# Output projection of ten token tiles in pairs by Strassen's scheme: seven block products for eight, block sums on GpSimd and VectorE

## The chip, the cores and the metric

The kernel runs on one core of a Trainium2 chip. A core has a matrix engine (TensorE, PE in the profile, with its weight loads listed apart as PEld), a vector engine (VectorE, DVE), an activation engine (ScalarE, ACT), GpSimd (POOL) and SyncE (SP), which here only issues transfers. SBUF is the on-chip memory of 128 partitions; PSUM is where TensorE writes, in eight banks that each hold 128x512 numbers in float32. The metric is the time of one execution on the device in microseconds, as the median of several runs.

## The reference

One decoder layer on 2048 tokens of width 1024. The input is normalised, projected once, and goes through two kinds of attention with eight heads each (a causal one with a forget gate, a sliding-window one). Each branch is multiplied by a SiLU gate path; the two halves of 512 columns are joined, sent through one output projection, normalised, and added to the input through a gate:

```
proj = h @ w_in[l]
qa, ka, va, fa, za, qb, kb, vb, zb = jnp.split(proj, split_points, axis=-1)
oa = forgetting_attention(qa, ka, va, fa + b_fgate[l])
oa = oa * jax.nn.silu(za)
...
ob = ob * jax.nn.silu(zb)
y = jnp.concatenate([oa, ob], axis=-1) @ w_out[l]
x = x + gate[:, None, :] * rms_norm(y, g_post[l])
```

All inputs and the output are float32.

## The kernel before

**Number format.** TensorE multiplies float16. Each float32 operand is scaled and split into a high and a low float16 limb, and a product is three matmuls: high by high, high by low, low by high. All of them add into one PSUM bank.

**Stages.** First the input is normalised and transposed, and the projections for the window attention run, with that attention beside them. Then comes the sweep of the forgetting attention: eight heads of 20 steps, 160 in all, each with scores (L1294 to L1297), an exponential (L1301), its split in limbs (L1305, L1308) and the product with the values (L1318 to L1321). Between the steps, in the same loop, the remaining projections are put in as filler. The gate projections za (for the forgetting attention) and zb (for the window attention) are evacuated by `evac_z` (L352): a Tanh on ACT, a multiply on DVE, and a transfer to `z_d` in DRAM from POOL's queue. `w_done` (L277) computes for each of the eight blocks of 128 columns the factor `fac8` by which its z is off. The attention results go to `o_d` in DRAM.

**Output projection.** It is done for 16 token tiles of 128 rows by the class `Out`. `load` brings o and z of a tile, `turn` (L1406) transposes o by eight PE transposes, multiplies it with z from the banks (`gate`, L1419), takes the sum of squares (L1423) and from it a scale (`root_scale`, L118, a power-of-two-like estimate of an inverse root with an exponent offset 15), and makes the high limb on ACT (L1437) and the low limb on DVE (L1438). `product(n, k)` (L1476) does one of eight k blocks of one half n of 512 output columns: three matmuls at L1489. After the eighth, `evac` multiplies the bank by the inverse scale and the gate row `gacc` on DVE (L1498) and sums its squares on ACT (L1499); after both halves, `root` and `store` (L1507 to L1519) finish the norm, add x and store the tile. The last half of the last tile is done in two pieces (`last`, L1440).

The weights `w_out` are loaded in 16 pieces during the sweep and split into limbs in `wohl` (`w_out_load`, `w_out_split`, L1387 and L1388), each row block scaled by `wsc`, which holds its `fac8` times a common factor. The right half's float32 pieces stay in `hT[3]`.

**Order.** The order within each engine is written out by hand. `ounits` is the list of units of the output projection, a unit being one `product` (three matmuls) or one `turn`; `ofill` runs them in turn. `after(n, f)` puts f off by n ticks, and outside the sweep a tick comes every second unit (`tick2`). 33 units (`N_IN`: both halves of tiles 0 and 1, and the turn of tile 2) are filler in the last head of the sweep; the rest follow the sweep at L1645. A tile's load is started two tiles ahead.

**Buffers.** Five PSUM banks `bk` take turns (`bank`, `release`); the sweep holds the other three. `Ts[0]` holds o and z of two tiles each in the tail, `Ts[1]` the limbs of the last head's q and k; `hT[2]` holds x and y of two tiles. The area for the descriptors of POOL's transfers has its default size.

Of the kernel before, what the change touches and what calls it, by code (L numbers as in the profile page):

```python
# [18 lines left out]
P = 128  # L19
# [22 lines left out]
def hybrid_layer(  # L42
# [75 lines left out]
    def root_scale(dst, ss):  # L118

        h = small.tile([P, 1], I32, tag="rs_h", name="sc_h")  # L120
        V.tensor_scalar(h[:], ss.bitcast(I32), 1, None, op0=ALU.logical_shift_right)
        V.tensor_scalar(dst.bitcast(I32), h[:], -1, 0x5F3759DF + (15 << 23), op0=ALU.mult, op1=ALU.add)
# [42 lines left out]
    fac8 = const.tile([P, KT], F32, name="fac8")  # L165
    wrt = const.tile([P, 1], F32, name="wrt")
# [986 lines left out]
    ps_st = fox_pool("ps_st", 1, space=PSUM)  # L1153
    ps_po = fox_pool("ps_po", 1, space=PSUM)
    ps_bx = fox_pool("ps_bx", 1, space=PSUM)
    bk += [ps_bx.tile([P, CH], F32, name=f"bk{n}") for n in (3, 4)]
# [198 lines left out]
    def open_out():  # L1355
# [7 lines left out]

        fm = sm(1, "w_p2")
        V.tensor_reduce(fm[:], fac8[:], axis=AX.X, op=ALU.max)
# [24 lines left out]
    oio = {}  # L1390

    class Out:
# [47 lines left out]
        def last(self, k):  # L1440
# [3 lines left out]
            if k == 0:  # L1444
                self.x = xy(self.t % 2)
# [30 lines left out]
        def product(self, n, k):  # L1476
# [3 lines left out]
            if k == 0:  # L1480
# [3 lines left out]
                else:  # L1484
                    self.x = xy(self.t % 2)
# [8 lines left out]
            def evac():  # L1494
                if n == 0:
                    self.y = xy(2 + self.t % 2)
# [23 lines left out]

    outs = [Out(t) for t in range(NB)]

    ounits, oloads = [], {}
    for t, n in [(0, 0), (1, 0), (0, 1), (1, 1)] + [(t, n) for t in range(2, NB) for n in range(2)]:
        if n == 0 and t + 2 < NB:
            oloads[len(ounits)] = t + 2
        for q in range(KT):
            ounits.append(lambda t=t, n=n, q=q: outs[t].product(n, q))
            nxt = 2 if (t, n) == (0, 1) else t + 1 if n == 0 and 2 <= t < NB - 1 else None
            if q == 2 and nxt:  # L1530
                ounits.append(lambda nxt=nxt: outs[nxt].turn(4))
    opos = [0]
    N_IN = 4 * KT + 1

    def ofill(n, each=None):
        for _ in range(n):
            if opos[0] in oloads:
                outs[oloads[opos[0]]].load()
# [5 lines left out]
    with tc.manual_schedule():  # L1544
# [30 lines left out]
        for s, stp_ in enumerate(steps):  # L1575
# [43 lines left out]
            if not opened and pos[0] >= N_OPEN and (r >= 14 or not late):  # L1619
# [8 lines left out]
                w_out_load(0)  # L1628
            if hd == 7 and r in (4, 6):
# [14 lines left out]
        fxs.close()  # L1644
        ofill(len(ounits) - opos[0], tick2)  # L1645
        for _ in range(4):
            tick()

    foxo.close()
# [32 lines left out]
```

## Time and profile before

| | |
|---|---|
| runs, us | 1195.15, 1192.07, 1190.61 |
| median of the runs, us | 1192.07 |
| span of the profiled execution, us | 1188.7 |
| PE busy in it, us (share) | 1147.3 (97%) |
| DVE busy, us (share) | 914.1 (77%) |
| ACT busy, us (share) | 665.9 (56%) |
| POOL busy, us (share) | 115.2 (10%) |

The profile is of one execution, whose span is 3.4 us under the median of the runs. A group of instructions is shown as line, engine, operation, output<-input, shapes and count, then the busy time in us and the mean duration of one in ns, then the idle time of the engine in front of them and what ended it. Matmuls are pipelined: one of 512 columns lasts some 380 ns from its start to its end, and the next starts before it is done, so the chain of waits, which follows the end of each, gives the time per matmul. "L1489" is a line of the kernel.

### The profile page before, as it was taken

To read this page: it belongs to the slowest core of one execution; us is meant where nothing else is said; L and a number is where in the kernel's file an instruction comes from. 1 tells how busy PE (TensorE), PEld (TensorE's weight loads), DVE (VectorE), ACT (ScalarE), POOL (GpSimd) and SP (SyncE) were. 2 spreads that over 40 slices of the span, in tenths; PEclk is the share of its full clock that TensorE was granted. 3 is DMA by queue.
4 is the path that set the end of the run, shared out by engine and by line. 5 is a ranking of instruction groups with operands and counts; after the bars stand their busy time and mean duration, and the time that the engine had idled before them with its cause. 6 is when DMAs were issued, how large, how long until landed. Compare 5 with 4: busy or idle time off the path is not lost.

```text
span 1188.7 us, 27244 instructions
## 1 busy us (share of the span) xinstructions
PE 1147.3 (97%) x10853; PEld 693.6 (58%) x10853; DVE 914.1 (77%) x2263; ACT 665.9 (56%) x1102; POOL 115.2 (10%) x231
## 2 busy tenths in 40 slices
PE   5899999999999998999999999999999999999997
PEld 2475556765558976555555555555555555555554
DVE  7876678687776748688888889887888887766665
ACT  2784345464655521476766667666666778433332
POOL 2000112212121211001000101001000000000000
PEclk9899999999999999999999999999999999999999
DMA  9745433314223322413325322212311345455642
GB/s 333 277 121 87 84 89 99 61 59 109 83 70 88 58 63 63 65 50 95 68 70 72 102 63 60 50 48 71 48 42 39 92 127 176 147 171 184 198 167 96
DMA packets 87579, 120.22 MB, mean 101 GB/s; under 512 B 27508, under 2 KB 63388, under 8 KB 87452
## 3 DMA queue, kind: packets, MB, share of 16 engines
q1 hardware_dynamic: 76184, 85.69, 24.4%
q0 software_dynamic: 10832, 32.50, 13.2%
q8 instruction: 85, 1.39, 0.6%
q14 instruction: 42, 0.34, 0.1%
q10 hardware_dynamic: 436, 0.28, 0.1%
HBM read 71.04 MB, written 25.18 MB: 81 GB/s over the span
## 4 chain that ended last, share of the span: by engine, by line
PE 79%; DVE 10%; DMA 6%; issue 2%; ACT 2%; SPq 1%; DVEq 0%; ACTq 0%
PE bk L317 29%; PE bk L1489 13%; PE bk L335 7%; PE sta L1295 4%; PE sta L1294 4%; PE bk L1245 4%; PE poa L1320 2%; PE poa L1321 2%; PE poa L1318 2%; DMA wa<-in_w_ada_dram 2%; PE pxb L888 2%; PE pss L855 2%; PE pob L907 2%; DVE a_m L1248 1%; PE bk L1410 1%
## 5 line engine op out<-in xcount | busy, mean ns | idle before, releaser
L1301 ACT ACTIVATE p<-sta,lift,scl_qk 128x1024 f32<-128x1024 f32 (+2 forms) x160 | 172.0, 1075 | 143.7 <-PE sta L1295 88.2
L317 PE MATMUL bk<-hT,wh_qk 128*128 128x512 f16 x768 | 195.3, 380 | 0.0
L1248 DVE TENSOR_REDUCE a_m<-bk 128x1 f32<-128x512 f32 x192 | 130.5, 686 | 55.2 <-PE bk L1245 54.0
L1308 DVE TENSOR_TENSOR pha<-p,pha 128x1024 f16<-128x1024 f32 (+2 forms) x160 | 169.1, 1057 | 0.2 <-ACT pha L1305 0.2
L1489 PE MATMUL bk<-wohl,oz 128*128 128x512 f16 x744 | 167.0, 379 | 0.7 <-DVE oz L1438 0.7
L1305 ACT ACTIVATE pha<-p 128x1024 f16<-128x1024 f32 (+2 forms) x160 | 148.1, 926 | 5.4 <-PE poa L1321 0.7
L1489 PEld LDWEIGHTS <-oz 128*128 128x128 f16 x744 | 71.9, 99 | 79.4 <-DVE oz L1438 2.8
L317 PEld LDWEIGHTS <-wh_qk 128*128 128x128 f16 x768 | 72.5, 98 | 78.2 <-issue 6.6
L1321 PE MATMUL poa<-vt,pha 128*128 128x65 f16 x1088 | 116.1, 192 | 1.4 <-DVE pha L1308 1.2
L1318 PE MATMUL poa<-vt,pha 128*128 128x65 f16 x1088 | 116.5, 193 | 0.5 <-DVE ona L1327 0.4
L1320 PE MATMUL poa<-vt,pha 128*128 128x64 f16 x1088 | 116.5, 194 | 0.0
L1245 PE MATMUL bk<-T 66*128 66x512 f16 (+2 forms) x320 | 110.2, 350 | 3.1 <-DVE a_m L1248 3.0
L1294 PE MATMUL sta<-T 128*128 128x512 f16 (+1 forms) x320 | 110.9, 346 | 2.5 <-ACT p L1301 2.4
L1318 PEld LDWEIGHTS <-pha 128*128 128x128 f16 x1088 | 101.5, 96 | 15.1 <-DVE ona L1327 1.5
L1295 PE MATMUL sta<-T 69*128 69x512 f16 (+1 forms) x320 | 109.8, 348 | 0.0
L1320 PEld LDWEIGHTS <-pha 128*128 128x128 f16 x1088 | 100.9, 97 | 11.4
L1321 PEld LDWEIGHTS <-pha 128*128 128x128 f16 x1088 | 100.8, 99 | 1.8 <-DVE pha L1308 1.7
L317 PE MATMUL bk<-hT,wh_za 128*128 128x512 f16 x384 | 99.7, 378 | 0.0
L335 PE MATMUL bk<-wh_va,hT 128*128 128x128 f16 x1536 | 90.7, 219 | 0.0
L335 PEld LDWEIGHTS <-hT 128*128 128x128 f16 x1536 | 87.5, 98 | 4.7 <-issue 2.1
L317 PE MATMUL bk<-hT,wh_zb 128*128 128x512 f16 x384 | 88.9, 379 | 0.0
L317 PE MATMUL bk<-hT,wh_qb 128*128 128x512 f16 x384 | 87.4, 379 | 0.0
(498 smaller groups left out, 1860.4 us busy)
## 6 DMA issues: line engine op xcount, KB each, us to landing
hT<-in_x_dram SPq DMA_DIRECT2D x20, 512.0 KB
wa<-in_w_ada_dram SPq DMA_DIRECT2D x16, 512.0 KB
z_d<-tz POOLq DMA_DIRECT2D x32, 256.0 KB, 2.9
T<-stq SPq DMA_DIRECT2D x64, 128.0 KB
T<-o_d SPq DMA_DIRECT2D x16, 512.0 KB
T<-z_d SPq DMA_DIRECT2D x16, 512.0 KB
out_dram<-hT SPq DMA_DIRECT2D x15, 512.0 KB
xt<-in_x_dram SPq DMA_DIRECT2D x12, 512.0 KB
```

The source lines that it names most:

```text
L317: PE.matmul(ps, whl[:, a, k, :], hT[ci][:, b, k, :], start=(k == 0 and n == 0), stop=(k == KT - 1 and n == 2))
L335: PE.matmul(ps[:, u * P:(u + 1) * P], hT[ci][:, a, k, u * P:(u + 1) * P], whl[:, b, k, :], start=(k == 0 and n == 0), stop=(k == KT - 1 an ...
L1245: PE.matmul(mx[:, :w], T[0:XM, 0, i * P:(i + 1) * P], T[0:XM, 2, pc * CH:pc * CH + w], start=True, stop=True)
L1294: PE.matmul(self.st[:, o:o + w], T[:, 3, kb_], T[:, 1, qc], start=True, stop=False)
L1295: PE.matmul(self.st[:, o:o + w], T[0:XR, 2, kb_], T[0:XR, 0, qc], start=False, stop=not diag)
L1301: A.activation(self.p32[:, :self.w], self.st[:, :self.w], AF.Exp, scale=scl[f"qk{self.hd}"][:], bias=lift[:])
L1305: A.activation(self.ph[:, 0, :self.w], self.p32[:, :self.w], AF.Copy)
L1308: V.tensor_tensor(self.ph[:, 1, :self.w], self.p32[:, :self.w], self.ph[:, 0, :self.w], op=ALU.subtract)
L1318: PE.matmul(po[:, u, :], ph[:, 0, pq], vt[:, b, hd, 0:65], start=(self.first and n == 0 and u == 0), stop=False)
L1320: PE.matmul(po[:, u, 0:64], ph[:, 0, pq], vt[:, b, hd, 65:VW], start=False, stop=False)
L1321: PE.matmul(po[:, u, :], ph[:, 1, pq], vt[:, b, hd, 0:65], start=False, stop=(self.last and n == len(self.blocks) - 1))
L1489: PE.matmul(py, self.hl[:, i, k, :], w_slot(8 * j + k)[:, cc], start=(k == 0 and m_ == 0), stop=(k == KT - 1 and m_ == 2))
```

## The change

Token tiles 4 to 13 are taken in five pairs. A pair is a 256 x 1024 matrix of gated attention results, cut into 2 x 2 blocks (tile 2p or 2p+1; first or second 512 of the inner columns), and `w_out` is cut into 2 x 2 blocks of 512 x 512. The eight block products become seven, in the form with seven sums after them:

- sums of the weights, once: T1 = B12 - B11, T3 = B22 - B12, T2 = B22 - T1, and T4 (with its sign turned), on POOL, 128x1024 at a time (`t_add`). For them the left half of `w_out` is loaded again into `Ts[1]` once the last scores are done (`t_load`), and the limbs of the four results are made by ACT and DVE (`t_high`, `t_low`) and kept where the values of the attention were.
- sums of the left side, per pair: four of 128x512 on POOL (`sums`).
- products 1, 2, 6, 7, 5, 3, 4 of four k blocks each, three matmuls per k block (`product` of the class `Two`).
- sums of the results: product 1 and 5 are copied from their banks by ACT; the others are added to a float32 row block by DVE; two sums that need only copies are made by POOL (`fives`). The gate row is multiplied in by POOL (`gated`) after the squares.

The sums over rows of z need both halves of the inner columns to have one scale per row of `w_out` blocks; so each za block is multiplied by the ratio `rat` of its factor to that of the matching zb block, by POOL, before it goes to `z_d`. Offsets 15 become 14 in `root_scale` since sums are larger. The tail gets the three banks that the sweep held. The descriptor area of POOL's transfers is set to 8192 bytes, which makes room for the new buffers. The units and what goes between them are listed at fixed unit numbers (`oat`).

```diff
-    def root_scale(dst, ss):
+    def root_scale(dst, ss, e=14):
...
-        V.tensor_scalar(dst.bitcast(I32), h[:], -1, 0x5F3759DF + (15 << 23), op0=ALU.mult, op1=ALU.add)
+        V.tensor_scalar(dst.bitcast(I32), h[:], -1, 0x5F3759DF + (e << 23), op0=ALU.mult, op1=ALU.add)
...
+            if kind == "za":
+                t = sm(1, "w_p2")
+                V.reciprocal(t[:], fac8[:, n + 4:n + 5])
+                V.tensor_tensor(rat[:, n:n + 1], fac8[:, n:n + 1], t[:], op=ALU.mult)
...
                 V.scalar_tensor_tensor(t[:], t[:], 1.0, ps, op0=ALU.add, op1=ALU.mult)
                 free()
+                if kt < 4:
+                    G.tensor_scalar(t[:], t[:], rat[:, kt:kt + 1], None, op0=ALU.mult)
                 G.dma_start(z_d[kt, :, ci * CH:(ci + 1) * CH], t[:])
...
-        V.tensor_scalar(wsc[:], fac8[:], ysc[:], None, op0=ALU.mult)
+        for n in range(2):
+            V.tensor_scalar(wsc[:, 4 * n:4 * n + 4], fac8[:, 4:8], ysc[:], None, op0=ALU.mult)
...
+    def t_add(n, h):
+
+        a = slice(h * 2 * CH, (h + 1) * 2 * CH)
+        b = slice((h + 2) * 2 * CH, (h + 3) * 2 * CH)
+        dst, x0, x1 = {1: (Ts1f[:, a], hT3f[:, a], Ts1f[:, a]), 3: (hT3f[:, a], hT3f[:, b], hT3f[:, a]),
+                       2: (hT3f[:, b], hT3f[:, b], Ts1f[:, a]), 4: (Ts1f[:, b], Ts1f[:, b], hT3f[:, b])}[n]
+        G.tensor_tensor(dst, x0, x1, op=ALU.subtract)
...
+        def sums(self):
...
+            G.tensor_tensor(c[:, 0:4], z1[:, 0:4], z1[:, 4:8], op=ALU.add)
+            G.tensor_tensor(f[:, 0:4], c[:, 0:4], z0[:, 0:4], op=ALU.subtract)
+            G.tensor_tensor(f[:, 4:8], z0[:, 0:4], z1[:, 0:4], op=ALU.subtract)
+            G.tensor_tensor(c[:, 4:8], z0[:, 4:8], f[:, 0:4], op=ALU.subtract)
...
+        def product(self, m, k):
+            n, half = {1: (0, 0), 2: (0, 1), 6: (1, 0), 7: (1, 1), 5: (2, 0), 3: (2, 1), 4: (3, 1)}[m]
...
+                PE.matmul(py, self.h[n][:, i, 4 * half + k, :], w,
+                          start=(k == 0 and m_ == 0), stop=(k == 3 and m_ == 2))
...
+        def add(self, dst, m, other):
+            V.tensor_tensor(dst, bk[self.bank[m]][:], self.u[other], op=ALU.add)
+            release(self.bank[m])
...
+        def fives(self):
+            G.tensor_tensor(self.u[2], self.u[15], self.u[2], op=ALU.add)
+            G.tensor_tensor(self.y(1, 1), self.u[15], self.u[3], op=ALU.add)
...
+        def gated(self, e, h):
+            G.tensor_tensor(self.y(e, h), self.y(e, h), gacc[:, h * CH:(h + 1) * CH], op=ALU.mult)
...
+    def prep(w):
+        i = len(ounits)
+        oat(i - 28, w.load)
+        for e in range(2):
+            oat(i - 18 + 2 * e, w.turn, e)
+            oat(i - 16 + 2 * e, w.gate, e)
+            oat(i - 14 + 2 * e, w.squares, e)
+        oat(i - 12, w.sums)
+        oat(i - 9, w.scale_)
+        for n, (a, b) in enumerate(((-7, -5), (0, 3), (6, 9), (12, 14))):
+            oat(i + a, w.high, n)
+            oat(i + b, w.low, n)
...
+    for n, h, at in ((1, 0, 6), (1, 1, 6), (3, 0, 8), (3, 1, 8), (2, 0, 22), (2, 1, 22), (4, 0, 26), (4, 1, 26)):
+        oat(N_IN + at, t_add, n, h)
+    for m, n in enumerate((1, 3, 2, 4)):
+        for k in range(4):
+            at = N_IN + (12, 20, 30, 38)[m] + 2 * k
+            oat(at, t_high, n, k)
+            oat(at + 1, t_low, n, k)
+    std(2, 0, 3)
...
+    for p in range(2, 7):
+        prep(twos[p])
+        for m in (1, 2, 6, 7, 5, 3, 4):
+            strassen(twos[p], m)
...
+            if s == len(steps) - 2:
+                t_load()
...
+        ps_tl = fox.enter_context(tc.tile_pool(name="ps_tl", bufs=1, space=PSUM))
+        bk += [ps_tl.tile([P, CH], F32, name=f"bk{n}") for n in (5, 6, 7)]
+        order_[:0] = [5, 6, 7]
...
-    nc = _bacc.Bacc("TRN2", target_bir_lowering=False, num_devices=1)
+    nc = _bacc.Bacc("TRN2", target_bir_lowering=False, num_devices=1, dynamic_dma_scratch_size=8192)
```

`std(t, n)` lists the eight units of one half of a tile as before. In `strassen(w, m)` the four units of product m are followed, one unit later, by its copy or sum, the square at three and the gate row at four; `root` comes six units after the last product, the two stores eight and ten after it.

More of the change, by code (lines that the diff above doesn't have):

```diff
@@ L165, in hybrid_layer @@
     fac8 = const.tile([P, KT], F32, name="fac8")
+    rat = const.tile([P, 4], F32, name="rat")
     wrt = const.tile([P, 1], F32, name="wrt")
@@ L1527, in hybrid_layer, with oat, std @@
+    outs = [Out(t) for t in range(NB)]
+    twos = {p: Two(p) for p in range(2, 7)}
+    ounits, oev = [], {}
+    def oat(n, f, *a):
+        oev.setdefault(n, []).append(lambda: f(*a))
+    def std(t, n, nxt=None):
         for q in range(KT):
[L1528 to L1529 removed]
+            ounits.append(lambda q=q: outs[t].product(n, q))
             if q == 2 and nxt:
[L1531 removed]
+                ounits.append(lambda: outs[nxt].turn(4))
@@ new lines, in prep, with strassen, end @@
+    def prep(w):
+        i = len(ounits)
+        oat(i - 28, w.load)
+        for e in range(2):
+            oat(i - 18 + 2 * e, w.turn, e)
[6 more added lines that the diff above has]
+            oat(i + b, w.low, n)
+    def strassen(w, m):
+        for k in range(4):
+            ounits.append(lambda k=k: w.product(m, k))
+        e = len(ounits)
+        def end(e_, h_):
+            oat(e + 3, w.square, e_, h_)
+            oat(e + 4, w.gated, e_, h_)
+        if m == 1:
+            oat(e + 1, w.copy, 1)
+        elif m == 2:
+            oat(e + 1, lambda: w.add(w.y(0, 0), 2, 11))
+            end(0, 0)
+        elif m == 6:
+            oat(e + 1, lambda: w.add(w.u[2], 6, 11))
+        elif m == 7:
+            oat(e + 1, lambda: w.add(w.u[3], 7, 2))
+        elif m == 5:
+            oat(e + 1, w.copy, 5)
+            oat(e + 1, w.load_x)
+            oat(e + 2, w.fives)
+            oat(e + 5, w.square, 1, 1)
+            oat(e + 6, w.gated, 1, 1)
+        elif m == 3:
+            oat(e + 1, lambda: w.add(w.y(0, 1), 3, 2))
+            end(0, 1)
+        else:
+            oat(e + 1, lambda: w.add(w.y(1, 0), 4, 3))
+            end(1, 0)
+            oat(e + 6, w.root)
+            oat(e + 8, w.store, 0)
+            oat(e + 10, w.store, 1)
```

156 lines of the change are left out of this document (143 added, 13 removed).

## The prediction

> **What bounds the kernel now.** I read the head of the page first, then the chain of waits, then the busy time of the engines in three stretches after the attention sweep.
>
> ```profile
> span 1188.7 us, 27244 instructions
> ...
> PE 1147.3 (97%) x10853; PEld 693.6 (58%) x10853; DVE 914.1 (77%) x2263; ACT 665.9 (56%) x1102; POOL 115.2 (10%) x231
> ```
> ```profile
> 600.00:700.00 100.00, 98.67 (x1022) 56.97 (x1018) 87.17 (x184) 65.36 (x75) 9.39 (x14) 1.00 0.36 73
> ...
> 1022.90:1047.60 24.70, 24.70 (x128) 12.63 (x126) 16.79 (x45) 7.60 (x14) 0.00 (x0) 1.00 0.66 216
> 1047.60:1161.30 113.70, 113.70 (x582) 58.28 (x581) 74.88 (x210) 37.99 (x70) 0.00 (x0) 1.00 0.56 186
> ```
>
> The columns are the stretch, its length, then the busy time of PE, PEld, DVE, ACT and POOL, the granted clock, the DMA share and GB/s. From 1022.9 us on only the output projection is left, and PE is busy all the time at the full clock. DVE works 66% of it, ACT a third, POOL not at all. So in this stage a matmul taken away is time taken away, as long as what replaces it stays under PE. The chain of waits, in order of time, gives the price of one tile:
>
> ```profile
> 1022.91 1.94 PE bk L1489 x9
> 1024.85 0.87 PE bk L1410 x8
> 1025.73 3.88 PE bk L1489 x18
> ...
> 1029.72 6.50 PE bk L1489 x30
> 1036.22 0.87 PE bk L1410 x8
> 1037.10 4.53 PE bk L1489 x21
> 1041.63 0.12 PE bk L1427 x2
> 1041.74 5.85 PE bk L1489 x27
> 1047.59 0.87 PE bk L1410 x8
> ...
> 1058.96 0.87 PE bk L1410 x8
> ```
>
> A matmul of 128x512 takes 6.50/30 = 0.2167 us of PE, the eight transposes of a tile 0.87 us, and two tiles 1058.96 - 1036.22 = 22.74 us, without a gap between the pieces.
>
> **What is removed.** A pair of tiles has 2 x 2 x 8 x 3 = 96 matmuls now. By the scheme it has seven products of four k blocks with three limb products each, 84. Five pairs save 60 matmuls of the same shape, 60 x 0.2167 = 13.0 us, and the count at L1489 and its successor together goes from 744 to 684. Transposes and the sum over partitions for the scale keep their number. A pair then needs 22.74 - 12 x 0.2167 = 20.1 us of PE. Tiles 0 to 3, 14 and 15 and the last 27 us of the kernel stay as they are.
>
> **What is added to DVE and ACT per pair.** The groups of the stretch from 1030 us to the end give the durations:
>
> ```profile
> L1498 DVE SCALAR_TENSOR_TENSOR hT<-bk,w_sw,gacc 128x512 f32<-128x512 f32 x27 | 20.1, 746 | 8.2 <-PE bk L1489 8.2
> L1499 ACT ACTIVATE yj<-bk,w_sw 128x512 bf16<-128x512 f32 x27 | 18.6, 687 | 72.8 <-DVE hT L1498 72.8
> L1438 DVE SCALAR_TENSOR_TENSOR oz<-T,w_pw,oz 128x1024 f16<-128x1024 f32 x13 | 16.7, 1282 | 6.5 <-ACT oz L1437 6.5
> L1518 DVE SCALAR_TENSOR_TENSOR hT<-hT,y_rs 128x1024 f32<-128x1024 f32 x13 | 16.5, 1272 | 0.0
> L1419 DVE TENSOR_TENSOR T<-bk,T 128x512 f32<-128x512 f32 x24 | 15.5, 686 | 19.5 <-PE bk L1410 19.5
> L1437 ACT ACTIVATE oz<-T,w_pw 128x1024 f16<-128x1024 f32 x13 | 14.9, 1142 | 1.0 <-DVE w_pw L122 1.0
> L1423 ACT ACTIVATE zj<-T 128x1024 bf16<-128x1024 f32 x12 | 12.7, 1056 | 25.6 <-issue 25.6
> ```
>
> and DVE's timeline (start, duration) shows the root of one tile, 1037.90 to 1040.03, and the four small instructions of the scale, 1041.78 to 1042.44:
>
> ```profile
> 1037.90 0.15 DVE L1509 TENSOR_TENSOR y_ss<-y_ss 128x1 f32<-128x1 f32 x1
> ...
> 1039.87 0.16 DVE L115 SCALAR_TENSOR_TENSOR y_rs<-rs_t,rs_y 128x1 f32<-128x1 f32 x1
> ...
> 1041.78 0.16 DVE L121 TENSOR_SCALAR sc_h<-bk 128x1 int32<-128x1 int32 x1 [0.66 <-PE bk L1427]
> ...
> 1042.44 1.27 DVE L1518 SCALAR_TENSOR_TENSOR hT<-hT,y_rs 128x1024 f32<-128x1024 f32 x1
> 1043.62 1.28 DVE L1438 SCALAR_TENSOR_TENSOR oz<-T,w_pw,oz 128x1024 f16<-128x1024 f32 x1
> ```
>
> DVE: four gates as L1419, 4 x 0.69 = 2.7; low limbs of three and a half tiles as L1438, 3.5 x 1.28 = 4.5; five sums of a bank with a row block, taken as L1419, 5 x 0.69 = 3.4 (the four evacuations of L1498, 3.0, go); two final instructions as L1518, 2.5; the scale 0.66; the root 2.1 now, with some four more small instructions at about 0.19, 2.9. Sum 16.7 us in 20.1. Starts at 1042.44 and 1043.62 lie 1.18 apart where one lasts 1.27, so back to back it is about a tenth of a microsecond less for each of these. ACT: two squares of L1423, 3.5 high limbs of L1437, two copies and four squares as L1499: 2.1 + 4.0 + 1.4 + 2.7 = 10.2 us, about half of the time. Both lie beside PE; DVE's cover is only 3.4 us a pair. DMA moves the same 4 MB per pair (two tiles of o, z, x and out) in 20.1 instead of 22.74 us, 186 x 22.74/20.1 = 210 GB/s, less than the 216 GB/s of the first stretch above.
>
> **What is added to POOL.** Ten two-input instructions of 128x512 a pair, eight of 128x1024 once (the T sums), and a scale of 128x512 for each of 16 z blocks during the sweep. The page of before shows no such instruction on POOL; the nearest rows among its groups are
>
> ```profile
> L508 POOL TENSOR_SCALAR_AFFINE_SELECT bmask<-bm 128x256 f32<-128x256 f32 x1 | 0.4, 401 | 0.1
> ...
> L511 POOL TENSOR_SCALAR_AFFINE_SELECT dm<-zero 128x128 f32<-128x128 f32 x1 | 0.3, 300 | 0.0
> ```
>
> That is 0.79 ns an element over 0.2 us. One input at 512 would be 0.6 us and at 1024 1.0 us, the lower end. I take twice the slope for two inputs, 1.0 and 1.8 us, because the second input must be read too; four times, 1.8 and 3.4 us, is my upper end. A pair then costs POOL 10 us, between 6 and 18, under 20.1 at every end. [...]
>
> What no row shows is how POOL and DVE get along when both read SBUF. If only DVE instructions with two SBUF inputs must take turns with POOL (low limbs 4.5 and finals 2.5, 7.0 us a pair), turns and all come to 10 + 7.0 = 17.0 us, still under PE; if every DVE instruction must, 16.7 + 10 = 26.7, over it. Both ends are kept; I take the first, with 0.4 us of PE stall a pair for a DVE that is late now and then, 2 us in all. [...]
>
> In the sweep DVE is busy 87% (row above) and 16 POOL scales of 0.6 us are spread over some 500 us. Wholly exposed they would be 16 x 0.6 = 10 us; DVE's idle 13% and the two tz buffers cover them, and I take 0.3 us. If the cover were gone, the next Tanh on ACT would wait for its tz. The smaller descriptor area for POOL's DMAs costs nothing unless they are held back; a weight load, by the DMA issues (count, KB, us to landing), lands in
>
> ```profile
> wr_qk<-in_w_in_dram POOLq DMA_DIRECT2D x16, 256.0 KB, 5.4
> ```
>
> and is issued 42 units (of three long matmuls, 0.65 us) ahead, so one or two in flight at a time is enough. The eight reciprocals and products for rat, and two small wsc instructions, go under DVE's idle time.
>
> **The first pair: the T sums.** The extra load of w_out (2 MB) waits for the last scores, and SP then has nothing queued in front; the timelines of PE and SP show the last scores and SP's next transfer:
>
> ```profile
> 1016.94 0.22 PE L1297 MATMUL sta<-dmaskT,identb 128*128 128x128 bf16 x1
> ```
> ```profile
> 1023.62 0.38 SPq L1328 DMA_DIRECT2D o_d<-ona  x1
> ```
>
> So it starts near 1017.2, and at 216 GB/s its first half is in SBUF about 5 us later, before POOL needs it near 1027. T1 and T3 are then done in 4 x 1.8 = 7 us, before ACT and DVE split them. What is tight is DVE. Per T block the splits cost what those of w_out cost:
>
> ```profile
> L1388 DVE SCALAR_TENSOR_TENSOR wohl<-hT,wsc,wohl 128x512 f16<-128x512 f32 x8 | 6.0, 748 | 4.7 <-ACT wohl L1387 4.7
> ```
> ```profile
> 1031.86 1.14 ACT L1437 ACTIVATE oz<-T,w_pw 128x1024 f16<-128x1024 f32 x1
> ```
>
> The first T high limb comes behind this ACT instruction (ends 1033.0) and its low limb on DVE near 1033.7. Up to the low limb that the first pair starts with stand eight T low limbs 6.0, tile 3's low limb 1.28, four gates 2.7, two evacuations 1.5, a root 2.1, a scale 0.66, and that limb itself 1.28: 15.5 us, so 1049.2, or about 1048 with the overlap of starts. PE gets there at 1022.91 + 96 x 0.2167 + 3 x 0.87 + 0.24 = 1046.6, and needs that limb in its third matmul, 1047.0. PE waits 1 to 2 us. Behind it on POOL the pair's sums stand ahead of T2 and T4; at 1.8 and 3.4 us an instruction T2 would come some 3 us late for the third product, at 1.0 and 1.8 in time. I take 2 us for this stage, between 0 and 6.
>
> **Sum.** 1188.7 - 13.0 + 2 + 2 + 0.3 = 1180.0 us of span. The median of the runs is 1192.07, 3.4 over the span, so 1183.4, rounded to 1183.5.
>
> **Rivals.** (1) *All hidden:* PE stays without gaps, as it is now through all 113.70 us, and nothing of the 4.3 us is paid: 1192.1 - 13.0 = 1179.1. For it speaks DVE's 3.4 us of air a pair; against it the 15.5 us queue before the first pair. Chance 0.20. (2) *The forecast,* 1180.5 to 1187: 0.45. (3) *DVE becomes the bound of the pairs:* POOL takes from it 3.4 us a pair and up to 3 more, so a pair lasts 20.1 to 23 us; with 4 us at the T sums 1183 to 1198, centre 1191. For it speaks that DVE would go from 66% to 83% with waits on POOL inside its queue (sums of the next pair stand on POOL ahead of the two fives, for which DVE's sum of the third product waits). Chance 0.18. (4) *DVE and POOL take turns in everything,* the other side: 26.7 us a pair against 22.74, 5 x 4.0 = 20 us, and at the T sums POOL's 8 x 1.8 = 14 us fall on DVE's queue, which is late already, some 10 of them on PE: 1192 + 30 = 1222, or 1200 if half of it is exposed. It decides from 6.0 us a pair (22.74 - 16.7), that is 0.6 us lost per POOL instruction. For it speaks only that no row excludes it. Chance 0.15. (5) *The change doesn't take matmuls away* (a count that stays at 744): 1192; the code leaves little room, 0.02.
>
> **How the numbers follow.** A measurement of this kernel tells about 0.5%, 6 us, from no change: faster is under 1186.1, slower over 1198. Faster: 0.20, nearly all of (2), 0.42, and 0.02 of (3), 0.64. Same: 0.03 of (2), 0.14 of (3), 0.02 of (5), 0.19. Slower: 0.15 of (4) and 0.02 of (3), 0.17. The range, 1177.5 to 1196, holds (1), (2) and most of (3); the forecast's own range is 1180.5 to 1187.
>
> **What would show it.** 684 matmuls of 512 columns at 0.217 us; a pair of 20.1 to 21 us from transposes to transposes; POOL instructions of 128x512 near 1.0 us; PE idle near 1047 released by DVE's low limb, 1 to 3 us; the sweep ending within 1 us of 1022.9. DVE rows as L1438 well over 1.3 us, or PE idle in every pair behind DVE, speak for (3); the same on L1419's kind, with a bank as input, for (4).

## The result and the profile after

Four runs of the changed kernel took 1226.43 to 1231.70 us, median 1228.88; four of the kernel before beside them 1190.61 to 1196.04, median 1193.61. The ratio is 1.0295 (95% interval 1.027 to 1.032): slower by 3%, where 1183.5 us had been forecast and 1177.5 to 1196 was the range. The head of the page of the profiled execution:

```profile
span 1226.0 us, 27290 instructions
## 1 busy us (share of the span) xinstructions
PE 1146.4 (94%) x10793; PEld 688.9 (56%) x10793; DVE 957.3 (78%) x2248; ACT 688.4 (56%) x1138; POOL 239.0 (19%) x305
```

Sixty matmuls are gone (10853 to 10793), 13 us at full clock, yet PE's busy time is less than 1 us under that of before, and the span is 37.3 us longer. In places the granted clock has fallen, to 0.87 in the first of the stretches below, so the same matmuls keep PE busy for longer. The busy times by stretch (columns as in the prediction; the first stretch is from the first matmul behind the sweep to the first product of the first pair, the others lie between the transposes of one pair and those of the next):

```profile
1027.30:1070.30 43.00, 26.10 (x127) 13.09 (x128) 34.68 (x51) 12.71 (x23) 21.59 (x11) 0.87 0.32 101
1079.90:1104.20 24.30, 20.88 (x105) 10.28 (x104) 18.02 (x31) 11.04 (x20) 14.40 (x10) 1.00 0.57 180
1104.20:1130.60 26.40, 22.35 (x105) 10.83 (x104) 19.68 (x43) 10.21 (x18) 14.67 (x11) 0.94 0.48 160
1130.60:1155.40 24.80, 22.26 (x106) 11.02 (x105) 17.34 (x34) 10.14 (x18) 14.47 (x10) 0.93 0.51 170
```

PE, busy without a break before, now stands still for 2 to 4 us in every pair, and no other engine is full: DVE has 17 to 20 us of work in 24 to 26, POOL 14.5, ACT 10 to 11. Where PE waits, its timeline says (three rows from the first stretch and just before it, with the idle time in front and its releaser):

```profile
1026.13 0.20 PE L1329 MATMUL poa<-vt,pha 128*128 128x65 f16 x1 [2.18 <-DVE pha L1316]
...
1037.43 0.38 PE L1440 MATMUL bk<-w_mx,ones 128*128 128x1 f32 x2 [3.30 <-ACT zj L1436]
...
1070.28 1.03 PE L1652 MATMUL bk<-wohl,oh 128*128 128x512 f16 x2 [12.44 <-ACT oh L1631]
```

and its groups behind the sweep show the place in the pairs, the sum over partitions for the scale (L1612):

```profile
L1612 PE MATMUL bk<-wst,ones 128*128 128x1 f32 x20 | 3.9, 263 | 13.7 <-ACT zj L1598 13.7
```

**The 12.44 us.** DVE's timeline in front of it is the root of a single tile, instructions of one number a partition:

```profile
1055.61 0.14 DVE L105 TENSOR_SCALAR rs_v<-rs_v 128x1 f32<-128x1 f32 x1
...
1056.39 2.27 DVE L115 SCALAR_TENSOR_TENSOR rs_y<-rs_t,rs_y 128x1 f32<-128x1 f32 x1
1058.70 2.26 DVE L110 SCALAR_TENSOR_TENSOR rs_t<-rs_y,rs_v 128x1 f32<-128x1 f32 x1
1060.99 2.26 DVE L115 SCALAR_TENSOR_TENSOR rs_y<-rs_t,rs_y 128x1 f32<-128x1 f32 x1
1063.29 2.26 DVE L110 SCALAR_TENSOR_TENSOR rs_t<-rs_y,rs_v 128x1 f32<-128x1 f32 x1
1065.58 0.16 DVE L115 SCALAR_TENSOR_TENSOR y_rs<-rs_t,rs_y 128x1 f32<-128x1 f32 x1
```
```profile
1056.30 4.64 POOL L1552 TENSOR_TENSOR hT<-hT,T 128x1024 f32<-128x1024 f32 x2
1060.90 4.63 POOL L1552 TENSOR_TENSOR T<-T,hT 128x1024 f32<-128x1024 f32 x2
```

An instruction of 0.16 us lasts 2.26. The starts are 2.3 us apart, the length of one of the four T sums that POOL runs at that time: one of DVE's, one of POOL's, in turn. Away from the sums the same lines last 0.16 to 0.22. The instruction at L105 reads one tensor, those that wait read two. Behind this root in DVE's queue stand the scale, a T low limb and an evacuation (L1513). For that evacuation ACT has stood still, and the first pair's high limb, for which PE waits, is behind it on ACT:

```profile
1067.80 0.69 ACT L1514 ACTIVATE yj<-bk,w_sw 128x512 bf16<-128x512 f32 x1 [15.02 <-DVE hT L1513]
...
1069.09 1.14 ACT L1631 ACTIVATE oh<-zx,w_pw 128x1024 f16<-128x1024 f32 x1
```

The other two waits in the list above are of the same kind. The last `pha` of the sweep (L1316, two inputs, 0.55 us as a rule) takes 2.12 while POOL is in the first T sum (2.18 us at 1026.13). Then a final instruction (L1533), a sum of squares (L1524) and one of the root (L110) last 2.25, 2.30 and 1.64 us in place of 1.28, 0.15 and 0.22, and the gate whose squares PE waits for stands behind them (3.30 us at 1037.43).

**The 13.7 us.** DVE and POOL in the fourth pair:

```profile
1151.18 1.88 DVE L1635 SCALAR_TENSOR_TENSOR oz<-sf,w_pw,oz 128x1024 f16<-128x1024 f32 x1 [1.37 <-ACT oz L1631]
1152.99 1.22 DVE L1686 TENSOR_TENSOR a_cv<-a_mr 128x2 f32<-128x2 f32 x1
...
1156.94 1.29 DVE L1693 SCALAR_TENSOR_TENSOR hT<-hT,a_m 128x1024 f32<-128x1024 f32 x1
1158.14 1.28 DVE L1635 SCALAR_TENSOR_TENSOR oz<-sf,w_pw,oz 128x1024 f16<-128x1024 f32 x1
...
1159.94 1.28 DVE L1693 SCALAR_TENSOR_TENSOR hT<-hT,a_m 128x1024 f32<-128x1024 f32 x1
...
1163.59 1.27 DVE L1594 TENSOR_TENSOR zx<-bk,zx 128x512 f32<-128x512 f32 x2
```
```profile
1163.70 0.38 PE L1612 MATMUL bk<-wst,ones 128*128 128x1 f32 x2 [0.57 <-ACT zj L1598]
1166.15 0.38 PE L1612 MATMUL bk<-wst,ones 128*128 128x1 f32 x2 [2.07 <-ACT zj L1598]
```

A low limb and the sum for the root wait for POOL (1.88 and 1.22 us), then come the root, two finals, limbs, and only then the gate of the pair's second tile. The squares follow it, and PE stands at the scale sum, with matmuls behind it that have all they need.

In front of these rows stands a second kind of wait, for POOL's results:

```profile
1147.36 0.69 DVE L1668 TENSOR_TENSOR hT<-bk,uc 128x512 f32<-128x512 f32 x1 [1.16 <-POOL uc L1677]
```
```profile
1148.59 0.72 ACT L1673 ACTIVATE yj<-hT,w_sw 128x512 bf16<-128x512 f32 x1 [3.77 <-POOL hT L1678]
```

DVE waits 1.16 us for a sum of `fives` in four of the five pairs. ACT waits for the other one, and behind ACT's squares stands the high limb for which the low limb at 1151.18 waits (1.37 us).

**Where the 37.3 us are.** The sweep's scores start and end at

```profile
L1294 PE MATMUL sta<-T x320: 217/379/381, 479.6 to 1016.8; 128*128 128x512 f16 x128, 128*128 128x256 f16 x32
```
```profile
L1302 PE MATMUL sta<-T x320: 217/379/380, 480.5 to 1018.9; 128*128 128x512 f16 x128, 128*128 128x256 f16 x32
```

(before, then after; the last two numbers in front of the semicolon): 0.9 us later at their start and 1.2 us longer over 538 us. From the last scores to the first matmul behind the sweep 2.3 us more (6.1 to 8.4); from there to the first pair 20.3 more (43.0 against 96 x 0.2167 + two tiles' transposes and scale, 22.7); the five pairs, from first product to first product, 11.4 more (125.1 against 113.7); the end 1.2. Sum 37.3. One tile's transposes, 0.87 us, have moved from the pairs into the stretch before them, which now holds three; against what PE needs there, 23.6 us, it is 19.4 us longer, 16.9 of waits (3.30, 1.16 and 12.44) and 2.5 of longer busy time.

### The profile page after: what moved, and what is told of

Its sections match the earlier page's. It is cut to its first block, busy times and chain, and to the rows that moved or that the text cites. A ratio compares the mean times of both kernels' runs of the same rounds, so it can differ in the third digit from the quotient of the medians.

```text
span 1226.0 us, 27290 instructions
## 1 busy us (share of the span) xinstructions
PE 1146.4 (94%) x10793; PEld 688.9 (56%) x10793; DVE 957.3 (78%) x2248; ACT 688.4 (56%) x1138; POOL 239.0 (19%) x305
## 5 line engine op out<-in xcount | busy, mean ns | idle before, releaser
L1316 DVE TENSOR_TENSOR pha<-p,pha 128x1024 f16<-128x1024 f32 (+2 forms) x160 | 170.5, 1065 | 0.2 <-ACT pha L1313 0.2
L1328 PEld LDWEIGHTS <-pha 128*128 128x128 f16 x1088 | 100.9, 97 | 11.4
L365 POOL TENSOR_SCALAR tz<-tz,rat 128x512 f32<-128x512 f32 x16 | 31.9, 1994 | 238.6 <-DVE tz L362 194.6
L1258 DVE CUSTOM_DVE_ANT_0 bk<-bk,cmask 128x128 f32<-128x128 f32 (+3 forms) x128 | 62.5, 494 | 6.6 <-PE bk L1253 6.3
```

Of the source, the lines that this page charges most:

```text
L1316: V.tensor_tensor(self.ph[:, 1, :self.w], self.p32[:, :self.w], self.ph[:, 0, :self.w], op=ALU.subtract)
L1328: PE.matmul(po[:, u, 0:64], ph[:, 0, pq], vt[:, b, hd, 65:VW], start=False, stop=False)
```

## The experiments

Each was run once, with the kernel before on the same chip (1192.3 to 1195.5 us). The place where the sweep ends differed by up to 5 us between kernels with the same or nearly the same sweep (first matmul behind it at 1024.0 to 1029.1), so the 2.1 us up to the last scores are no more than such differences, and beside the time I compare three stretches: the *stage* from the first matmul behind the sweep to the first product of the first pair, the *pairs* from there to the first product of tile 14, and the *tail*, all from the first matmul behind the sweep to the end. After: stage 43.0, pairs 125.1, tail 198.7. Before the tail is 165.8, and with 60 matmuls less and nothing else it would be 152.8, with 23.6 in the stage and 113.7 - 13.0 - 0.9 = 99.8 in the pairs. Theory A, in most of the expectations: a DVE instruction with two tensors in SBUF waits for a whole GpSimd instruction, and all that stands behind it in DVE's queue waits with it. The others are named where they come.

### What DVE's small instructions wait for

**Small instructions with one tensor input.**

```diff
-                V.scalar_tensor_tensor(t[:], y[:], y[:], v[:], op0=ALU.mult, op1=ALU.mult)
+                V.tensor_scalar(t[:, c_:c_ + 1], yc, yc, v[:, c_:c_ + 1], op0=ALU.mult, op1=ALU.mult)
```

> Edit: only the small DVE instructions (root of a tile or a pair, sum of its two squares, inverse scale) change form: one tensor and one or two column scalars in place of two tensors. POOL's work stays. Theory A (a DVE instruction with two tensors in SBUF waits for the whole POOL instruction in progress, however small it is itself, and this holds back the T stage): the small ones that lasted 0.57 to 2.30 us between 1029 and 1066 us go back to 0.15 to 0.24 us, PE's gap of 12.4 us before the first pair falls under 5, and the time falls by 8 to 13 us, to about 1218. Rival B (POOL holds back every DVE instruction, or DVE's 12 us of T limbs are the load that is late): the small ones stay long or the gap stays, within 3 us of 1229.

1223.79 us; stage 32.3, pairs 129.3, tail 193.0. DVE and POOL at the T sums:

```profile
1053.73 0.27 DVE L112 TENSOR_SCALAR rs_t<-rs_y,rs_v 128x1 f32<-128x1 f32 x1
...
1055.99 2.15 DVE L1567 SCALAR_TENSOR_TENSOR vt<-hT,wsc,vt 128x512 f16<-128x512 f32 x1
...
1060.32 2.88 DVE L1567 SCALAR_TENSOR_TENSOR vt<-hT,wsc,vt 128x512 f16<-128x512 f32 x1 [1.51 <-ACT vt L1564]
1063.12 3.36 DVE L1641 SCALAR_TENSOR_TENSOR oh<-zx,w_pw,oh 128x1024 f16<-128x1024 f32 x1
```

The root runs through beside POOL at 0.15 to 0.27 us an instruction, and the stage is 10.7 us shorter, so it is the second tensor that waits, not the engine, and rival B falls. PE's gap of 12.44 us is down to 2.91. But the limbs that follow (0.75 and 1.28 us alone) now meet the sums, and PE waits 4.25 us for the low limb two matmuls on: the pairs are 4.2 us longer, and the time has come down by 5.1 us and not by 8 to 13.

**T sums cut in four.** `t_add` in four pieces of 128x256.

> Edit: each T sum on POOL of 128x1024 is cut into four of 128x256, same elements. Theory A (a small DVE instruction waits for one POOL instruction): the small ones that lasted 2.27 us last 0.5 to 0.8 us, and the time falls by 5 to 10 us. Rival B (POOL's work as such takes the time, however it is cut): no change, or slower by POOL's extra fixed cost, about 24 x 0.2 = 5 us on POOL.

1221.77 us; stage 36.8, pairs 126.9. The root's instruction waits for one piece, 0.65 us, and the pieces cost POOL more in all than the whole ones (eight in 5.94 us for two in 4.64):

```profile
1054.03 0.65 DVE L115 SCALAR_TENSOR_TENSOR rs_y<-rs_t,rs_y 128x1 f32<-128x1 f32 x1
1054.71 0.65 DVE L110 SCALAR_TENSOR_TENSOR rs_t<-rs_y,rs_v 128x1 f32<-128x1 f32 x1
```

That is 0.74 us a piece. Between these two kernels the wait goes by the length of the POOL instruction (2.26 us beside sums of 2.3, 0.65 beside pieces of 0.74), not by DVE's own (0.16 and 0.22 for these lines). PE waits 0.61 us for the last `pha`, in place of 2.18.

### What the GpSimd work costs

**Without the T sums.** The eight instructions at L1552 are left out, so the products with T aren't the layer's.

> Edit: the eight T sums on POOL are left out, so the products with T take unsummed weights; their limbs on ACT and DVE stay. Theory A: no POOL instruction meets the roots of tiles 1 and 2 and the last low limb of the sweep; 15 to 22 us less, 1207 to 1214. Rival B (the load of T limbs on DVE, which stays): less than 5 us, above 1224.

1214.34 us, at the upper end of theory A's range; stage 31.2, pairs 125.2, tail 186.9: 11.8 us of the stage were the T sums, and the pairs don't care.

**Without GpSimd in the pairs.** Nothing at L1604 to L1607, L1677, L1678 and L1681; limbs of z itself.

> Leaves out of the five pairs the ten GpSimd instructions of 128x512 (block sums, the two sums with the fifth product, the gates of the row blocks): the limbs are made of z itself, the fifth product is copied to its place by ScalarE, and the output isn't the layer's. The T sums stay. Theory A (instructions of GpSimd make DVE's wait, and DVE's queue is in order): the pairs fall from 23 to 27 us to 20.1 to 21, 125 to 101-105 in all, and the time to 1203-1209. Theory D (DVE's own longer list and the places of its instructions hold the pairs, GpSimd or not): the pairs stay at 22 to 24.5 us, time 1217-1226.

1209.0 us; stage 40.8, pairs 108.8, tail 180.2. A mixed answer: 16.3 us of the pairs were GpSimd's, but they are not at the 101 to 105 of theory A. The run takes away both the turns and the waits for POOL's results, so it doesn't divide the 16.3 between the two.

**Without GpSimd behind the sweep.** Both together.

> As the run without GpSimd in the pairs, and the T sums are left out too (T limbs from unsummed blocks), so nothing of GpSimd is left behind the sweep; matmuls, limbs, evacuations, roots and finals are all there. Theory A: also 12 to 15 us less in front of the first pair, time 1188-1195, the stretch from the first matmul behind the sweep to the end 157-163 us where the work on TensorE alone would take 152.8. Theory D: 1200-1212, stretch over 168 us.

1195.3 us; stage 29.0, pairs 108.8, tail 168.4. The tail is that of theory D, the time just beyond that of theory A: without GpSimd most of the loss is gone, but not all. The two costs add up (11.8 again at the stage), 30.3 us in all. The pairs now differ among themselves:

```profile
1035.30:1063.80 28.50, 22.86 (x105) 10.62 (x103) 20.85 (x42) 17.23 (x30) 0.00 (x0) 0.94 0.36 125
1063.80:1089.60 25.80, 22.32 (x104) 10.93 (x105) 19.07 (x47) 11.29 (x20) 0.00 (x0) 0.93 0.53 169
1089.60:1109.90 20.30, 20.30 (x106) 10.49 (x105) 15.29 (x35) 10.37 (x18) 0.00 (x0) 1.00 0.61 207
1109.90:1130.10 20.20, 20.20 (x105) 10.46 (x104) 15.18 (x35) 10.37 (x18) 0.00 (x0) 1.00 0.63 208
```

From the third on a pair takes 20.2 to 20.3 us, PE without a gap. The first two are slow with no GpSimd at all: there DVE and ACT still make the T limbs. From first product to first product it is the first pair alone, 28.95 us where PE needs 20.2. Groups of DVE in the pairs, of the kernel after

```profile
L1686 DVE TENSOR_TENSOR a_cv<-a_mr 128x2 f32<-128x2 f32 x4 | 4.9, 1221 | 0.0
...
L1615 DVE TENSOR_TENSOR w_sw<-w_pw,ysc 128x1 f32<-128x1 f32 x4 | 2.3, 569 | 0.1
```

and of this one

```profile
L1610 DVE TENSOR_TENSOR w_sw<-w_pw,ysc 128x1 f32<-128x1 f32 x4 | 0.6, 160 | 0.1
L1680 DVE TENSOR_TENSOR a_cv<-a_mr 128x2 f32<-128x2 f32 x4 | 0.6, 154 | 0.0
```

show two small instructions that lost 4.3 (the sum for the root) and 1.7 us (the scale); the low limbs of the same window lost 5.5 (20 of them, 28.4 against 22.9 us by their groups). With a bank as one input nothing was lost: the gates (L1594) mean 0.68 us in both.

**All sums on DVE.** `V.tensor_tensor` for `G.tensor_tensor` in `t_add`, `sums`, `fives`, `gated`.

> All sums and gates of the change on DVE in place of GpSimd (T sums too), same result. At 0.75 us a 128x512 with two inputs in SBUF (as its low limbs) DVE gets 10 x 0.75 = 7.5 us a pair on top of 16 to 17, about 24, and 8 x 1.28 = 10 us at the T sums. Theory A (a GpSimd instruction takes about its own length from DVE, so moving the work gains or loses little): 24 to 25.5 us a pair, 1215-1232. Theory D (DVE is full as it is): 26 us a pair and more, 1235-1250. If GpSimd's lateness alone is what costs (the sums come late, DVE itself loses nothing): under 1212.

1211.44 us; stage 35.2, pairs 116.9, tail 184.3. It lies under the range of theory A and just inside the third case, by which only the lateness of GpSimd's results costs. That DVE itself loses nothing is contradicted by the rows above (4.3, 1.7 and 5.5 us lost), but how much of the pairs' loss is lateness this run doesn't tell either. Moving the work back to DVE gains 14.4 us of tail, so a GpSimd instruction takes more from the pair than DVE's own time for it. The same instructions, first on POOL (pairs of the kernel after), then on DVE (this run, from the sweep to the end):

```profile
L1681 POOL TENSOR_TENSOR hT<-hT,gacc 128x512 f32<-128x512 f32 x18 | 27.0, 1517 | 51.7 <-ACT yj L1673 51.7
L1677 POOL TENSOR_TENSOR uc<-pc,uc 128x512 f32<-128x512 f32 x5 | 10.3, 2056 | 3.5 <-ACT pc L1664 3.5
```
```profile
L1681 DVE TENSOR_TENSOR hT<-hT,gacc 128x512 f32<-128x512 f32 x20 | 13.7, 686 | 2.7 <-ACT yj L1673 2.7
...
L1677 DVE TENSOR_TENSOR uc<-pc,uc 128x512 f32<-128x512 f32 x5 | 3.4, 678 | 0.0
...
L1552 DVE TENSOR_TENSOR hT<-hT,T 128x1024 f32<-128x1024 f32 x2 | 2.4, 1217 | 0.0
```

DVE does in 0.69 us what takes POOL 1.5 to 2.1 beside it (its block sums of the same size, L1604 to L1607, have means of 1.27). Over the tail without any sums, 168.4, the sums cost 15.9 us on DVE and 30.3 on POOL: handing them to the free engine made them twice as dear.

### Mending the order

**Square of the fifth product's block later** (`oat(e + 9, w.square, 1, 1)` for `e + 5`, its gate likewise), for the theory that ACT, standing at that square, holds up the limbs.

> Edit: square and gate row of the block y(1,1) of a pair, which wait for POOL's second sum of the fives, move four units back, behind the next pair's high limb of its first sum, on ACT and POOL. Theory C (a loop over the queues holds the pairs at 23 to 27 us: gate, POOL sums, POOL fives, square on ACT, high limb behind it, low limb, root and stores on DVE, next gate): pairs of 20.5 to 22 us, 8 to 14 us less, about 1218. Rival D (DVE is simply full with POOL's turns): pairs stay within 0.5 us, time within 3 us of 1229.

1227.41 us, pairs 123.5. ACT no longer waits for POOL there, and only 1.6 us come of it, so as the cause of the long pairs that theory falls.

**Finals later** (`oat(e + 18, w.store, 0)`, `e + 20` for `e + 8`, `e + 10`), so that the gates come first.

> Edit: the two final instructions and stores of a pair move from 8 and 10 to 18 and 20 units behind its last product, so that on DVE they stand behind the next pair's gates and not in front. Theory E (in the pairs PE waits for the scale sum, because the next pair's gate comes late on DVE behind low limbs, root and stores): the two waits of about 2 us a pair before the sum over partitions shrink by the 2.4 us of the two finals, pairs of 21 to 22.5 us, about 8 us less, near 1221. Rival D (DVE is full with POOL's turns, wherever its work stands): pairs stay, time within 3 us of 1229.

1224.04 us, pairs 122.2: 2.9 us of the pairs, between theory E's 8 and theory D's nothing.

**Both of these, with the one-input small instructions.**

> Edits together: small DVE instructions with one tensor, late square of y(1,1), late finals. If the turns of small instructions and the order on DVE are two separate causes, the gains add: pairs of 20.3 to 21.5 us and a T stage 9 us shorter, 1203 to 1211. Rival (each only moves the wait to the next engine): 1216 or more.

1218.62 us; stage 32.3, pairs 126.5. The rival holds: the stage keeps the gain of the one-input instructions, 10.7 us, and the pairs gain nothing. In three of them DVE now waits 2.38 or 2.39 us for POOL's `uc` sum, where it was 1.16.

**And T2, T4 right behind T3 on POOL.**

> The kernel labelled pairs_mended, and T2 and T4 stand on POOL right behind T3, ahead of the first pair's sums. Theory: in the kernel labelled one_input the low limbs of T and of the first pair lasted 2.15 to 3.36 us between 1056 and 1066 because they met T2 and T4; with those over by about 1046 they last 0.75 and 1.28 and the first pair starts some 5 us earlier: 5 us less than pairs_mended. Rival: the limbs of T1 and the finals of tile 1 meet the T sums instead, no gain over 1.5 us.

1216.12 us; stage 35.5, pairs 124.8. The 2.5 us gained are not the theory's: the tail is 190.4 against 188.9, and the sweep ended 4.0 us earlier. The wait right before the first pair is gone (0.03 us in place of 2.92), but others have grown in front of it. The rival, no gain, holds.

**And tiles 4 and 5 one by one**, so four pairs, the T limbs spread over 46 units.

> The kernel labelled t_sums_first with four pairs (tiles 6 to 13), tiles 4 and 5 one by one, and the 16 pairs of T limb instructions spread over 46 units in place of 34. It saves 48 matmuls, 10.4 us, not 60. Theory (DVE's 12 us of T limbs do not fit beside two tiles, each of which leaves it 3.5 us, but fit beside four): PE idle before the first pair under 1.5 us, and the time is 2 to 8 us under t_sums_first, perhaps under the kernel before. Rival (the T limbs fit anyway): 2.6 us slower than t_sums_first.

1211.22 us; stage 60.4 (two single tiles more, about 22.7), pairs 90.5, or 22.6 each: as long as two single tiles before. It is 4.9 us under the version before it and PE waits 1.43 us before the first pair, both as the theory had it, though 8.4 us of other waits lie in the stage.

**And the pairs' root one column at a time.** In that version two one-input instructions of 128x2 still waited:

```profile
L103 DVE TENSOR_SCALAR rs_h<-rs_v 128x2 int32<-128x2 int32 x3 | 3.6, 1197 | 0.1
L98 DVE TENSOR_SCALAR rs_v<-a_cv 128x2 f32<-128x2 f32 x3 | 2.6, 858 | 0.1
```

> The version with four pairs, with the pair's root made one column at a time, so that no small DVE instruction has two elements a partition. Theory A: the 128x2 ones that took up to 1.2 us beside GpSimd take 0.15-0.25 us, 2 to 4 us of DVE a pair, time 1203-1209, still over the kernel before. If those waits lay under TensorE's work anyway: 1209-1213, as four_pairs.

Now they read

```profile
L103 DVE TENSOR_SCALAR rs_h<-rs_v 128x1 int32<-128x1 int32 x7 | 1.1, 153 | 0.2
...
L98 DVE TENSOR_SCALAR rs_v<-a_cv 128x1 f32<-128x1 f32 x6 | 0.9, 143 | 0.0
```

and the time is 1210.54 us, pairs 90.7. The waits were real, and lay under other waits: the second case.

### What is left without GpSimd

**Gates and squares four units earlier.**

```diff
-            oat(i - 18 + 2 * e, w.turn, e)
-            oat(i - 16 + 2 * e, w.gate, e)
-            oat(i - 14 + 2 * e, w.squares, e)
-        oat(i - 12, w.sums)
+            oat(i - 18 - s + 2 * e, w.turn, e)
+            oat(i - 16 - s + 2 * e, w.gate, e)
+            oat(i - 14 - s + 2 * e, w.squares, e)
+        oat(i - 12 - s, w.sums)
```

with s = 4 (2 in the first pair, and the loads 4 earlier but for that pair). On the kernel after:

> Only the places change: transposes, gates, squares and block sums of a pair 4 units (2.6 us of TensorE) earlier (2 for the first pair), the scale sum where it was. Theory L (TensorE stops at the scale sum because DVE's gates come just too late for it): the waits there (0.5 to 2.0 and 2.07 us a pair) go, pairs 112-118 us in place of 125.1, time 1216-1222. Theory F (DVE is full beside GpSimd): the wait turns up at the low limbs or elsewhere, pairs 121-126, time 1224-1230.

1220.59 us; stage 41.2, pairs 121.3: the time is in theory L's range, the pairs in theory F's. On the kernel without GpSimd:

> The kernel without GpSimd's work behind the sweep (block sums, T sums, gates of row blocks left out) with the same earlier places. Theory L: pairs 102-105 us in place of 108.8, time 1188-1192. Theory T (T limbs on DVE and ScalarE make the first two pairs late wherever the gates stand): pairs 107-110, the stretch before them 28-30 as before, time 1194-1197.

1191.09 us; stage 28.5, pairs 104.9, tail 163.9: theory L. And on the one with all sums on DVE:

> All sums and gates on DVE, with the same earlier places. DVE is busy 20.3 us a pair where nothing waits (window 1097.8-1119.1 of all_dve), TensorE 20.1. Theory L: pairs 104-109 in place of 116.9, time 1198-1205. Theory F: 114-117, time 1207-1212.

1211.85 us; stage 35.3, pairs 115.6: theory F. The lead takes 3.9 us out of the pairs without any sums, 3.8 with the sums on POOL and 1.3 with them on DVE. Only without sums does that bring the pairs to where theory L had them; with sums on either engine there are still waits. On DVE the reason is plain:

```profile
1116.50:1138.60 22.10, 20.61 (x106) 10.48 (x105) 21.17 (x45) 10.52 (x19) 0.00 (x0) 1.00 0.57 191
1138.60:1160.70 22.10, 20.62 (x106) 10.49 (x105) 21.16 (x45) 10.52 (x20) 0.00 (x0) 1.00 0.42 143
```

DVE is busy 21.2 of 22.1 us, so DVE sets the pair, 0.6 us less than two single tiles.

**Three pairs, T work spread over six single tiles, all on DVE.**

> As dve_early, but only tiles 8 to 13 are in pairs; tiles 2 to 7 go one by one and the T sums and limbs are spread over 79 units of theirs. On TensorE alone that is 165.8 - 3 x 2.6 = 158.0 us behind the sweep. If the T work is what loads the stretch before the pairs, it hides under the six single tiles (DVE has 34% of 68 us = 23 us free, the T work takes 22): 159-165 us, time 1185-1191. If DVE can't take it there: 168-174 us, time 1194-1200.

1203.39 us, over both ranges; stage 80.3 (four single tiles more, 45.5), pairs 62.5 or 20.8 each, tail 174.0. The pairs are nearly PE's (20.2), but the T sums and limbs make DVE late in the single tiles as well: PE waits 6.3 us there for their low limbs (L1451). It is the fastest of the versions that compute the layer, and still 11 us over the kernel before it ran beside. Nothing here points to one that beats it: with no sums at all and the better order five pairs have a tail of 163.9, 1.9 us under that of before, and their sums cost 15.9 us at the least. T sums made ahead of the sweep's end were not tried; their buffers are in use until then.

## Why the prediction was wrong

**The saving was right.** 684 matmuls at L1503 and L1652, and where nothing waits a pair takes 20.2 us (predicted 20.1). Sweep and z scales were nearly right too: 1.2 us over the sweep, for 0.3, and kernels with the same sweep differ by more.

**The step that failed is the cost of the sums on POOL**, "turns and all come to 10 + 7.0 = 17.0 us, still under PE ... with 0.4 us of PE stall a pair, 2 us in all". Three things in it:

- *The price of a turn.* It added busy times: 7.0 us for DVE's limbs and finals, as if a DVE instruction that meets POOL cost its own length. In the traces it costs the rest of POOL's instruction, also where its own length is 0.16 us: 2.26 us against sums of 2.3, 0.65 against pieces of 0.74. The small two-input instructions, costed at 0.15 to 0.22 by their rows, became the dearest: four of them 9.05 us in front of the first pair. Counted by the traces' lengths, the three groups above lose 4.3 + 1.7 + 5.5 = 11.5 us of DVE's time over the pairs, and leaving GpSimd out there gave 16.3 us of span. For the stage the runs show this step as the cause (T sums left out 11.8 us, one tensor in place of two 10.7, pieces 6.2). For the pairs they show that GpSimd's work costs 16.3, and rows in which DVE waits; how much of it comes by the turns and how much by POOL's late results, for which the forecast charged nothing either, stays open. That only DVE instructions with two SBUF inputs take turns, and the 0.4 us of PE stall a pair taken with it, were the author's choice between two ends; no run of before shows either. The runs after it showed the gates with a bank as input at 0.68 us with GpSimd and without, two-input instructions of 0.16 us at up to 2.26, and pairs of 125.1 us in place of 101.8.
- *Slack as an average.* "3.4 us of air a pair" is an average over a queue in order. DVE has its limb, root and finals of one pair in one block and the next pair's gates behind it, the last of them 5 units ahead of the sum for which PE stops, its squares 3. So PE waits about 2 us there, pair after pair, while DVE works 17 to 20 us of the 23 to 26. The prediction asked what DVE's work sums to, and not which instruction ends last before L1612.
- *The sums' own length.* 1.27 us at 512 columns against the 1.0 taken, 2.3 at 1024 against 1.8. That alone is small (inside the ends 0.6 to 1.8 and 1.0 to 3.4).

**The T stage**, "I take 2 us for this stage, between 0 and 6", came to 19.4. 11.8 are the T sums, 2.2 GpSimd's work for the first pair (43.0 to 40.8); the other 5.4 remain without GpSimd, where DVE and ACT make the T limbs; 1 to 2 had been worked out for them. By PE's rows of that run 2.9 of the 5.4 are waits at the first pair's scale sum (0.79 and 2.07), 0.2 one at its first product, and 2.3 longer busy time at a clock of 0.94. The prediction queued the T limbs on DVE alone, with ACT's part counted for the first limb only; in the run without GpSimd DVE waits 2.56 us once and 1.46 to 1.52 four times for ACT's high limb (L1558). How much of the 5.4 comes of that, no run separates. T2 "in time" at 1.0 and 1.8 us an instruction was the wrong question: the sums came in time and stopped others.

**The pairs** were taken at 99.8 + 2; they took 125.1. Of the 23.3 over that, GpSimd's work has 16.3; 3.9 are the short lead of the gates without it; the rest of 3.1 was not taken apart. The last `pha`, 2.3 us, was foreseen nowhere: the prediction had POOL begin the T sums near 1027, behind the sweep, and they began at 1023.32, inside it. With 1.2 at the end and 2.1 up to the last scores, the 46.0 us between the span of the forecast (1180.0) and 1226.0 are accounted for, less the 0.3 that it had for the sweep.

**The rivals.** (3), DVE the bound of the pairs, had named the place but priced it at 1183 to 1198. (4), 1200 to 1222, was nearest in time and wrong in its mechanism: instructions with a bank as one input don't wait (L1594 0.68 us), and "every DVE instruction" isn't needed, since a few wait for so long. That its time was near is luck. The prediction's first case, turns for two SBUF inputs alone, was the right one but for a few one-input instructions, and charged with POOL's length in place of DVE's it would have come to a loss: 11.5 us in the pairs and 9.05 in front of them, against 13.0 saved.

**Lost clock.** Some waits cost more than their length. In the windows of the kernel without GpSimd the two pairs in which PE is idle for 5.6 and 3.5 us have a granted clock of 0.94 and 0.93 and 2 us more of busy PE for the same work (22.86 and 22.32 against 20.3). Not all do: the pair at 1079.90 of the kernel after kept 1.00 with 3.4 us idle. The prediction charged every stall at its own length.

## What to carry to other kernels

Before work goes to GpSimd, list every DVE instruction with two SBUF tensors that can run beside it, the one-column ones above all, and charge each up to the length of a whole GpSimd instruction (2.26 us for 0.16 here). Set that against DVE's own time for the same sum (0.69 us here, against 1.27 to 2.1): it says whether the move pays. An engine's spare time per stage is no cover for a chain: look at what stands between the late instruction and the matmul that waits, and how far ahead it was issued. And a saving on the first bound is worth what the second leaves: with its sums DVE needs 22.1 us a pair, which leaves 0.6 of the 2.6 that PE saves, before the T work is paid.

## What the runs showed that was not expected

- DVE's one-input instructions are not all free of GpSimd: at 128x2 two of them (L98, L103) lasted 0.86 and 1.20 us beside it and 0.17 each in the kernel without it, at 128x1 0.14 to 0.15. L104 and L105 of the same width, at 0.16 to 0.17, say nothing against it: in that kernel (four pairs) GpSimd's last instruction ends at 1116.74, L103 just behind it at 1116.78, and L104 starts at 1116.81.
- GpSimd waits in turn: in the pairs an add of 128x512 takes it 1.27 us at L1604 to L1607 and 2.25 at the four of L1677 that meet a low limb of DVE (1.27 at the fifth, 2.06 on average), and its one-input scaling of 128x512 in the sweep takes 1.55 to 2.47 us beside a DVE that is busy 87% of the time from 512.7 to 984.0; no run shows that scaling alone:

```profile
L365 POOL TENSOR_SCALAR tz<-tz,rat 128x512 f32<-128x512 f32 x16 | 31.9, 1994 | 238.6 <-DVE tz L362 194.6 <-DVE a_ri L1333 44.0
```

- The granted clock fell in most stretches where PE had stood still, 0.87 over the stage with the 12.44 us gap, but not by the length of the wait: 0.94 in a stage with waits of 0.79 and 2.07 us on both sides of a small matmul (kernel without GpSimd), 1.00 with 3.27 us at 1091.47 (kernel after). What makes it fall, no run here settles.
